# A hybrid decoder layer on one core: the norms' inverse root as one GpSimd power operation

## The chip, the core and the metric

The kernel runs on one core of one Trainium2 chip. A core has five engines that run side by side and wait for each other by semaphores: TensorE (PE in the profile; PEld is its weight load), VectorE (DVE), ScalarE (ACT), GpSimd (POOL) and SyncE (SP), which here issues the transfers. The metric is the device time of one execution in microseconds (us). Three timed executions of the kernel before gave 1698.07, 1702.21 and 1703.12 us, so a median of 1702.21 us.

## The reference

One decoder layer for 1024 tokens of width 1024, in float32. Every sub-layer starts with an RMS norm, whose reciprocal root is what the change is about:

```python
def rms_norm(x, gain):
    y = x * lax.rsqrt(jnp.mean(x * x, axis=-1, keepdims=True) + EPS)
    return y * gain
...
h = modulate(rms_norm(x, ffn1_norm), sh1, sc1)
x = x + 0.5 * g1 * swiglu(h, w_gate, w_up, w_down)           # FFN 1
h = modulate(rms_norm(x, mix_norm), sh2, sc2)
b, c, v, u = split(h @ w_in)
y_conv = b * conv3_causal(c * v)
y_ssm = glu(s5_scan(u))
x = x + g2 * (concat(rms_norm(y_conv), rms_norm(y_ssm)) @ w_out)
h = modulate(rms_norm(x, ffn2_norm), sh3, sc3)
x = x + 0.5 * g3 * swiglu(h, w_gate2, w_up2, w_down2)        # FFN 2
return rms_norm(x, final_norm)
```

The shifts, scales and gates (`sh`, `sc`, `g`) come from `silu(cond) @ w_mod + b_mod`, nine vectors of 1024.

## The kernel before

**Layout.** Activations stand transposed: 128 features on the partitions, tokens along the free axis, in two halves `h` of 512 tokens. A float32 product is made from three TensorE products of a high and a low part (`mm3`, L337): high by high, high by low, low by high. ScalarE makes the high part (a cast), VectorE the low part (a subtraction), for weights and activations alike. Most FFN products use a seven-product scheme (`seven`, `down7`); GpSimd makes the sums of weights for it (L168 to L179).

**Order of the work.** TensorE's matmuls stand in program order, and a clock counts them: each `mm3` is one tick, and work that is due later is put on the clock with `clock.after(ticks, ...)`. VectorE, ScalarE, TensorE and SyncE go through the wrapper `InOrder`, so all their instructions carry line L112 in the profile; GpSimd's carry their own lines. Within an engine the order of issue is fixed when the program is built; a scheduler decides it outside the first stage, where `InOrder.strict` holds the order as written.

**The norms.** There are thirteen roots, each for up to four groups of 128 tokens:

- `p0`, `p1`: the first norm. Tokens are on the partitions there; `root_of` (L873) makes the root of four token blocks at once, `scaled` multiplies the blocks by it on ScalarE (half 1 partly on GpSimd), `turned` transposes them on TensorE.
- `n2a`, `n2b` (before the mixer), `nAa`, `nAb`, `nBa`, `nBb` (the conv group's and the SSM group's output norm), `n3a`, `n3b` (before FFN 2) and three for the final norm, of half 0 (`n_0` in the profile, from `n4`) and of the two halves of half 1. For these, `Sumsq.rstd` (L385) puts three pieces on the clock: TensorE sums the squares over the partitions (`...st`), `roots` (L400) makes the root and `wide` (L415) spreads it over 128 columns (`...rb`); seven ticks later (11 in the final norm) TensorE brings it to all partitions (`...bc`), and the users multiply by it.

`roots` is nine VectorE instructions on 128x4 (or 128x2) elements: `v` = mean square plus epsilon; a first guess from the bits of `v` read as an integer; and seven more for two refinements, whose last leaves 8/3 of the root. `wide`, or in `root_of` one more instruction, multiplies by 0.375.

**Other work on VectorE around the norms.** The modulation vectors of later sub-layers are made beside the main work: `wm` tiles of 128x1024 come by transfer into two buffers, and VectorE reduces each with one long instruction (`mod_vector`, L437), which in the mixer's last part writes `mods` and `gate`. A buffer is loaded again only once that instruction has read it. In the stage of the output projection (`w_out`, tiles `wo`), VectorE also makes `obt` (the SSM output times its root and gain), the low parts `ob`, the updates of `x` and the low parts of the weights `w`.

**Padding.** `PAD` sets the sizes of two unused tiles at the two ends of the local memory, and with them the addresses of what lies between.

Of the kernel before, what the change touches and what calls it, by code (L numbers as in the profile page):

```python
# [21 lines left out]
P = 128  # L22
D = 1024
# [18 lines left out]
GB = G // NB  # L42


PAD = 96, 100

C_BMOD, C_N1, C_N2, C_N3, C_NF, C_ONC, C_ONS, C_CW, C_GB = 0, 72, 80, 88, 96, 104, 108, 112, 124
NCOLS = 128
# [4 lines left out]
RC2 = float(np.float32(np.round((TWO_PI - RC1) * 2.0**20) / 2.0**20))  # L53
RC3 = float(np.float32(TWO_PI - RC1 - RC2))
ROUND = 12582912.0
ROOT_BITS, ROOT_A, ROOT_B = 1595932665.0, 0.703952253, 2.38924456
EXP_C = [1.9875691500e-4, 1.3981999507e-3, 8.3334519073e-3, 4.1665795894e-2, 1.6666665459e-1, 5.0000001201e-1]


# [176 lines left out]
def hymba_layer(ctx: ExitStack, tc, x_d, xt_d, wm1_d, wmod_d, gu1_d, gs1_d, ds1_d, wl1_d, win_d, wout_d, glu_d, gu2_d, gs2_d, wd2_d, ds2_d, wl2_d, cols_d, cond_d, lam_d, bc_d, out_d):  # L236
    nc = tc.nc
    V, A, T, SP = (InOrder(tc, e) for e in (nc.vector, nc.scalar, nc.tensor, nc.sync))

    def pool(name, bufs=1, **kw):  # L240
        return ctx.enter_context(tc.tile_pool(name=name, bufs=bufs, **kw))

    pad = pool("pad")
    pad.tile([P, PAD[0]], F32, name="pad_left")
    const = pool("const", side="right")
    const.tile([P, PAD[1]], F32, name="pad_right")
    scratch = pool("scratch", space=DRAM)
# [24 lines left out]
    def t2k(name):  # L272
        return tmp.tile([P, HALF], F32, tag="t", name=name)
# [3 lines left out]
    make_identity(nc, ident[:])  # L277
    one = const.tile([P, 1], F32, name="one")
    V.memset(one[:], 1.0)
    mods = const.tile([P, 3, KT], F32, name="mods")  # L280
    scl = const.tile([P, 3, KT], F32, name="scl")
    gate = const.tile([P, 3, KT], F32, name="gate")
# [111 lines left out]

            clock.after(wait, stats)

    def roots(st, q, width, nm):

        v, y, a = (const.tile([P, 8], F32, tag=f"n{i}", name=f"{nm}n{i}", bufs=1)[:, :q] for i in "vya")
        yi = const.tile([P, 8], I32, tag="ni", name=nm + "ni", bufs=1)[:, :q]  # L400
        V.tensor_scalar(out=v, in0=st[:, :q], scalar1=1.0 / width, scalar2=EPS, op0=ALU.mult, op1=ALU.add)
        V.tensor_scalar(out=yi, in0=v.bitcast(I32), scalar1=-0.5, scalar2=ROOT_BITS, op0=ALU.mult, op1=ALU.add)
        src = yi.bitcast(F32)
        V.scalar_tensor_tensor(out=a, in0=src, scalar=-ROOT_A, in1=src, op0=ALU.mult, op1=ALU.mult)
        V.tensor_tensor(out=a, in0=a, in1=v, op=ALU.mult)
        V.scalar_tensor_tensor(out=y, in0=a, scalar=ROOT_A * ROOT_B, in1=src, op0=ALU.add, op1=ALU.mult)
        V.tensor_tensor(out=a, in0=y, in1=y, op=ALU.mult)
        V.tensor_tensor(out=a, in0=a, in1=v, op=ALU.mult)
        V.scalar_tensor_tensor(out=a, in0=a, scalar=-10.0 / 3.0, in1=a, op0=ALU.add, op1=ALU.mult)
        V.scalar_tensor_tensor(out=y, in0=a, scalar=5.0, in1=y, op0=ALU.add, op1=ALU.mult)  # L410
        return y

    widened = []
# [1 line left out]
    def wide(y, nm):  # L415

        q = y.shape[1]
        rb = t2k(nm + "rb")[:, : q * P].rearrange("p (a b) -> p a b", a=q)
        r = V.tensor_scalar(out=rb, in0=y.unsqueeze(2).to_broadcast([P, q, P]), scalar1=0.375, scalar2=None, op0=ALU.mult)
        widened.append(r)  # L420
        return rb

# [399 lines left out]
    st = t2k("st")  # L822
# [1076 lines left out]
```

## Time and profile before

| what | value |
|---|---|
| median of the runs | 1702.21 us (1698.07 to 1703.12) |
| the profiled execution's span, and its own time by the profile | 1704.7 us |
| mean granted TensorE clock in it | 0.994 |
| PE busy | 1666.8 us (98%) |
| DVE busy | 1255.5 us (74%) |
| ACT busy | 630.1 us (37%) |
| POOL busy | 382.0 us (22%) |
| share of the chain that ended last | PE 70%, DVE 8%, DMA 5% |

The page's first part gives for each engine its busy time, its share of the span and the number of its instructions. A row of the timeline reads: start, duration, engine, line, operation, output from inputs, shapes, count of merged instructions, and in brackets how long the engine had been idle before it and what it had waited for. A busy TensorE hides what the others do, so the places to look at are those where it stands idle.

### The profile page before, as it was taken

To read this page: it belongs to the slowest core of one execution; us is meant where nothing else is said; L and a number is where in the kernel's file an instruction comes from. 1 tells how busy PE (TensorE), PEld (TensorE's weight loads), DVE (VectorE), ACT (ScalarE), POOL (GpSimd) and SP (SyncE) were. 2 spreads that over 40 slices of the span, in tenths; PEclk is the share of its full clock that TensorE was granted. 3 is DMA by queue.
4 is the path that set the end of the run, shared out by engine and by line. 5 is a ranking of instruction groups with operands and counts; after the bars stand their busy time and mean duration, and the time that the engine had idled before them with its cause. 6 is when DMAs were issued, how large, how long until landed. Compare 5 with 4: busy or idle time off the path is not lost.

```text
span 1704.7 us, 20844 instructions
## 1 busy us (share of the span) xinstructions
PE 1666.8 (98%) x7545; PEld 1369.9 (80%) x7545; DVE 1255.5 (74%) x1957; ACT 630.1 (37%) x1064; POOL 382.0 (22%) x297
## 2 busy tenths in 40 slices
PE   8999999999999999999999999999999999999997
PEld 5888877788878888788777878888888888888886
DVE  7897899998589978735555857957767667576655
ACT  6525323333354332331113415434344434322233
POOL 1012222242222412100000021122333223333212
PEclk9999999999999999999999999999999999999999
DMA  8544454544665448244654232324443343759212
GB/s 350 187 148 137 172 189 155 183 149 139 213 216 170 151 152 291 70 111 149 191 151 134 70 129 112 112 74 182 188 174 148 148 173 148 269 228 381 110 50 99
DMA packets 101625, 281.48 MB, mean 165 GB/s; under 512 B 19345, under 2 KB 34961, under 8 KB 90386
## 3 DMA queue, kind: packets, MB, share of 16 engines
q1 hardware_dynamic: 101522, 280.15, 46.6%
q8 instruction: 59, 0.97, 0.2%
q14 instruction: 44, 0.36, 0.1%
HBM read 195.69 MB, written 76.02 MB: 159 GB/s over the span
## 4 chain that ended last, share of the span: by engine, by line
PE 70%; DVE 8%; DMA 5%; issue 1%; ACT 0%; SPq 0%; POOL 0%; DVEq 0%; ACTq 0%; POOLq 0%
PE wo L112 4%; PE fald L112 3%; PE fb10d L112 2%; PE u L112 2%; PE fbd_1B L112 2%; PE fbd_0B L112 2%; DMA swz<-si 2%; DVE w L112 2%; PE fad_1B L112 2%; PE b L112 2%; PE fad_0B L112 1%; PE c L112 1%; PE fb0u L112 1%; PE fad_1C L112 1%; PE fbd_1C L112 1%; PE fbd_0C L112 1%
## 5 line engine op out<-in xcount | busy, mean ns | idle before, releaser
L112 ACT CAST w<-raw 128x512 fp32r<-128x512 f32 (+1 forms) x374 | 240.9, 677 | 497.7 <-issue 72.7
L112 DVE TENSOR_TENSOR w<-raw,w 128x512 fp32r<-128x512 f32 (+1 forms) x374 | 311.2, 851 | 101.2 <-ACT w L112 100.6
L177 POOL TENSOR_TENSOR raw<-sums,raw 128x512 f32<-128x512 f32 x54 | 81.6, 1511 | 420.9 <-DVE w L112 419.9
L168 POOL TENSOR_TENSOR sums<-raw 128x512 f32<-128x512 f32 x54 | 76.4, 1415 | 308.1 <-DMA raw<-in_ds 129.1
L179 POOL TENSOR_TENSOR raw<-raw 128x512 f32<-128x512 f32 x54 | 82.3, 1526 | 86.6 <-DVE w L112 86.0
L112 DVE CUSTOM_DVE_ANT_0 wm<-wm,cact 128x1024 f32<-128x1024 f32 x56 | 77.7, 1407 | 15.1 <-DMA wm<-in_wmod 15.0
L169 POOL TENSOR_TENSOR raw<-raw 128x512 f32<-128x512 f32 x54 | 85.2, 1577 | 4.2
L370 POOL TENSOR_TENSOR n3aq<-n3aq,n3aq 128x512 f32<-128x512 f32 x5 | 7.5, 1499 | 277.4 <-ACT n3aq L112 277.2
L112 DVE TENSOR_TENSOR w<-sums,w 128x512 fp32r<-128x512 f32 x54 | 54.9, 1029 | 3.4 <-ACT w L112 2.8
L112 PE MATMUL p<-h,w 128*128 128x512 f32 x192 | 49.4, 407 | 2.0 <-ACT h L112 1.5
L112 PE MATMUL wo<-oa,w 128*128 128x512 f32 x192 | 45.5, 391 | 2.1 <-ACT w L112 1.3
L112 PE MATMUL c<-h,w 128*128 128x512 f32 x192 | 47.1, 397 | 0.0
L112 PE MATMUL v<-h,w 128*128 128x512 f32 x192 | 46.9, 395 | 0.0
L112 PE MATMUL b<-h,w 128*128 128x512 f32 x192 | 45.6, 393 | 0.0
L112 PE MATMUL wo<-ob,w 128*128 128x512 f32 x192 | 45.2, 391 | 0.0
L112 PE MATMUL u<-h,w 128*128 128x512 f32 x192 | 44.8, 392 | 0.2 <-DVE h L112 0.2
L112 PEld LDWEIGHTS wo<-oa,w 128*128 128x128 f32 x192 | 35.8, 188 | 10.2 <-ACT w L112 1.7
L112 PEld LDWEIGHTS p<-h,w 128*128 128x128 f32 x192 | 35.7, 192 | 10.1 <-ACT h L112 2.0
L112 ACT CAST w<-sums 128x512 fp32r<-128x512 f32 x54 | 32.7, 619 | 28.8 <-PE fa10gE L112 2.5
L112 PEld LDWEIGHTS u<-h,w 128*128 128x128 f32 x192 | 35.7, 188 | 8.3 <-DVE h L112 0.6
L112 PEld LDWEIGHTS wo<-ob,w 128*128 128x128 f32 x192 | 35.8, 188 | 7.4
L112 PEld LDWEIGHTS c<-h,w 128*128 128x128 f32 x192 | 35.8, 190 | 7.2
(1579 smaller groups left out, 4039.8 us busy)
## 6 DMA issues: line engine op xcount, KB each, us to landing
raw<-in_gs SPq DMA_DIRECT2D x38, 1024.0 KB, 5.0
wm<-in_wmod SPq DMA_DIRECT2D x56, 512.0 KB, 5.2
raw<-in_ds SPq DMA_DIRECT2D x16, 1024.0 KB, 6.6
mw<-in_wm SPq DMA_DIRECT2D x8, 1024.0 KB, 8.4
raw<-in_win SPq DMA_DIRECT2D x8, 1024.0 KB, 5.5
raw<-in_gu SPq DMA_DIRECT2D x6, 1024.0 KB, 4.9
raw<-in_wl SPq DMA_DIRECT2D x5, 1024.0 KB, 6.7
xb<-in_xt SPq DMA_DIRECT2D x8, 512.0 KB, 6.4
```

The source lines that it names most:

```text
L112: r = getattr(self.engine, name)(*args, **kw)
L168: self.G.tensor_tensor(out=f, in0=r[2], in1=r[1], op=ALU.subtract)
L169: self.G.tensor_tensor(out=r[1], in0=r[1], in1=r[0], op=ALU.subtract)
L177: self.G.tensor_tensor(out=r, in0=s["t3"], in1=r, op=ALU.add)
L179: self.G.tensor_tensor(out=r, in0=self.chunk(j, 3), in1=r, op=ALU.subtract)
L370: nc.gpsimd.tensor_tensor(out=a, in0=a, in1=sq[:, :n], op=ALU.add)
```

## The change

The nine instructions of `roots` become two: `v` on VectorE as before, and one GpSimd `tensor_tensor` that raises `v` to the power -0.5, with a tile of constants as its second input. The factor 0.375 in `wide` becomes 1.0. In the first norm the GpSimd instruction writes the tile that `scaled` reads, so that the tenth instruction goes too. The three working tiles that fall away and the new tile of constants are balanced by `PAD`: the tiles `w`, `h` and the other matmul operands keep their addresses, while `cols` and `ident` move by 32 bytes.

```diff
-PAD = 96, 100
+PAD = 96, 108
...
+    power = const.tile([P, 4], F32, name="power")
+    nc.gpsimd.memset(power[:], -0.5)
...
-    def roots(st, q, width, nm):
-        v, y, a = (const.tile([P, 8], F32, tag=f"n{i}", name=f"{nm}n{i}", bufs=1)[:, :q] for i in "vya")
-        yi = const.tile([P, 8], I32, tag="ni", name=nm + "ni", bufs=1)[:, :q]
+    def roots(st, q, width, nm, y=None):
+        v = const.tile([P, 8], F32, tag="nv", name=nm + "nv", bufs=1)[:, :q]
+        if y is None:
+            y = const.tile([P, 8], F32, tag="ny", name=nm + "ny", bufs=1)[:, :q]
         V.tensor_scalar(out=v, in0=st[:, :q], scalar1=1.0 / width, scalar2=EPS, op0=ALU.mult, op1=ALU.add)
-        V.tensor_scalar(out=yi, in0=v.bitcast(I32), scalar1=-0.5, scalar2=ROOT_BITS, op0=ALU.mult, op1=ALU.add)
-        src = yi.bitcast(F32)
-        V.scalar_tensor_tensor(out=a, in0=src, scalar=-ROOT_A, in1=src, op0=ALU.mult, op1=ALU.mult)
-        V.tensor_tensor(out=a, in0=a, in1=v, op=ALU.mult)
-        V.scalar_tensor_tensor(out=y, in0=a, scalar=ROOT_A * ROOT_B, in1=src, op0=ALU.add, op1=ALU.mult)
-        V.tensor_tensor(out=a, in0=y, in1=y, op=ALU.mult)
-        V.tensor_tensor(out=a, in0=a, in1=v, op=ALU.mult)
-        V.scalar_tensor_tensor(out=a, in0=a, scalar=-10.0 / 3.0, in1=a, op0=ALU.add, op1=ALU.mult)
-        V.scalar_tensor_tensor(out=y, in0=a, scalar=5.0, in1=y, op0=ALU.add, op1=ALU.mult)
+        nc.gpsimd.tensor_tensor(out=y, in0=v, in1=power[:, :q], op=ALU.pow)
         return y
...
-        r = V.tensor_scalar(out=rb, in0=y.unsqueeze(2).to_broadcast([P, q, P]), scalar1=0.375, scalar2=None, op0=ALU.mult)
+        r = V.tensor_scalar(out=rb, in0=y.unsqueeze(2).to_broadcast([P, q, P]), scalar1=1.0, scalar2=None, op0=ALU.mult)
...
     def root_of(h):
-        y = roots(st[:, 4 * h : 4 * h + 4], 4, D, f"p{h}")
         root[h] = t2k(f"py{h}")[:, :4]
-        V.tensor_scalar(out=root[h], in0=y, scalar1=0.375, scalar2=None, op0=ALU.mult)
+        roots(st[:, 4 * h : 4 * h + 4], 4, D, f"p{h}", root[h])
```

The order in which instructions stand on the engines changes at few places beyond the removed rows. Three of them matter below. The first is VectorE around the second root of the conv group (`nAb`); `yg` are the low parts of the gate's input. Before:

```order
L112 TENSOR_SCALAR nAbnv<-nAbst 128x4
L112 TENSOR_SCALAR nAbni<-nAbnv 128x4
L112 SCALAR_TENSOR_TENSOR nAbna<-nAbni 128x4
L112 TENSOR_TENSOR nAbna<-nAbna,nAbnv 128x4
L112 SCALAR_TENSOR_TENSOR nAbny<-nAbna,nAbni 128x4
L112 TENSOR_TENSOR nAbna<-nAbny 128x4
```

The three further instructions of the root follow, then seven `yg` and the widening. In the changed kernel:

```order
L111 TENSOR_SCALAR nAbnv<-nAbst 128x4
L111 TENSOR_TENSOR yg_0_7407<-yb_7256,yg_0_7407 128x512
L111 TENSOR_TENSOR yg_0_7416<-yb_7257,yg_0_7416 128x512
L111 TENSOR_TENSOR yg_0_7425<-yb_7258,yg_0_7425 128x512
L111 TENSOR_TENSOR yg_1_7479<-yb_7255,yg_1_7479 128x512
L111 TENSOR_TENSOR yg_1_7485<-yb_7256,yg_1_7485 128x512
L111 TENSOR_TENSOR yg_1_7494<-yb_7257,yg_1_7494 128x512
L111 TENSOR_TENSOR yg_1_7509<-yb_7258,yg_1_7509 128x512
L111 TENSOR_SCALAR nAbrb<-nAbny 128x512
```

The low parts `yg` now stand right behind `v`, with no part of the root between them; the widening that waits for GpSimd stays behind all seven.

The second place is VectorE behind the second root of the SSM group (`nBb`); ISA rows are the long reductions of `wm` and the short read of their sum. Before:

```order
L112 TENSOR_SCALAR nBbrb<-nBbny 128x512
L112 ISA wm_2_0_7980,mods<-wm_2_0_7980,cact_7300 128x1024
L112 ISA mods 128x1
L112 SCALAR_TENSOR_TENSOR x_0_3914<-wo_0_7644,gate,x_0_3914 128x512
L112 SCALAR_TENSOR_TENSOR x_0_3914<-wo_0_7645,gate,x_0_3914 128x512
L112 ISA wm_2_1_7982,mods<-wm_2_1_7982,cact_7300 128x1024
L112 ISA mods 128x1
L112 SCALAR_TENSOR_TENSOR obt_1_7901<-yb_7293,cols,nBbbc 128x512
```

In the changed kernel:

```order
L111 TENSOR_SCALAR nBbnv<-nBbst 128x4
L111 TENSOR_SCALAR nBbrb<-nBbny 128x512
L111 ISA wm_2_0_7906,mods<-wm_2_0_7906,cact_7262 128x1024
L111 ISA mods 128x1
L111 ISA wm_2_1_7908,mods<-wm_2_1_7908,cact_7262 128x1024
L111 ISA mods 128x1
L111 SCALAR_TENSOR_TENSOR x_0_3894<-wo_0_7588,gate,x_0_3894 128x512
L111 SCALAR_TENSOR_TENSOR x_0_3894<-wo_0_7589,gate,x_0_3894 128x512
L111 ISA wm_3_0_7911,mods<-wm_3_0_7911,cact_7262 128x1024
L111 ISA mods 128x1
L111 SCALAR_TENSOR_TENSOR obt_1_7827<-yb_7255,cols,nBbbc 128x512
```

Every reduction from here to the end of this stage stands one place earlier: three reductions instead of two stand ahead of the first `obt`. On SyncE, correspondingly, one load of `wm` stands ahead of a load of weights that it stood behind.

The third place is VectorE in the last 20 us, from the root of half 1's first piece (`n_1_0`) on; `fb10d` are the last products. Before:

```order
L112 TENSOR_SCALAR n_1_0nv<-n_1_0st 128x2
L112 SCALAR_TENSOR_TENSOR x_1_3920<-fb10d_1_256_13389,gate,x_1_3920 128x256
L112 TENSOR_SCALAR n_1_0ni<-n_1_0nv 128x2
L112 TENSOR_TENSOR x_0_3916<-x_0_3916,n_0_0bc 128x1024
L112 SCALAR_TENSOR_TENSOR n_1_0na<-n_1_0ni 128x2
L112 SCALAR_TENSOR_TENSOR x_1_3921<-fb10d_1_256_13429,gate,x_1_3921 128x256
L112 TENSOR_TENSOR n_1_0na<-n_1_0na,n_1_0nv 128x2
L112 TENSOR_TENSOR x_0_3917<-x_0_3917,n_0_0bc 128x1024
L112 SCALAR_TENSOR_TENSOR n_1_0ny<-n_1_0na,n_1_0ni 128x2
L112 SCALAR_TENSOR_TENSOR x_1_3921<-fb10d_1_256_13449,gate,x_1_3921 128x256
```

In the changed kernel:

```order
L111 TENSOR_SCALAR n_1_0nv<-n_1_0st 128x2
L111 SCALAR_TENSOR_TENSOR x_1_3900<-fb10d_1_256_13288,gate,x_1_3900 128x256
L111 TENSOR_SCALAR n_1_0rb<-n_1_0ny 128x256
L111 TENSOR_TENSOR x_0_3896<-x_0_3896,n_0_0bc 128x1024
L111 SCALAR_TENSOR_TENSOR x_1_3901<-fb10d_1_256_13319,gate,x_1_3901 128x256
L111 TENSOR_TENSOR x_0_3897<-x_0_3897,n_0_0bc 128x1024
L111 SCALAR_TENSOR_TENSOR x_1_3901<-fb10d_1_256_13339,gate,x_1_3901 128x256
L111 TENSOR_TENSOR x_1_3898<-x_1_3898,n_1_0bc 128x2x256
L111 TENSOR_SCALAR n_1_256nv<-n_1_256st 128x2
L111 TENSOR_TENSOR x_1_3899<-x_1_3899,n_1_0bc 128x2x256
L111 TENSOR_SCALAR n_1_256rb<-n_1_256ny 128x256
```

The widening of the first piece stood behind the last update of `x` before and stands two updates ahead of it now; of the four multiplications by its result one instead of two stands ahead of the second piece's `v`, and one fills the place between `v` and its widening.

TensorE's order differs in two spots: the broadcast `n2bbc` stands behind six matmuls since its sum instead of ten, and the first `wo<-ob` of half 1 are taken in an order that runs two high-by-high products ahead of the first low part.

More of the change, by code (lines that the diff above doesn't have):

```diff
@@ L55 @@
 ROUND = 12582912.0
-ROOT_BITS, ROOT_A, ROOT_B = 1595932665.0, 0.703952253, 2.38924456
 EXP_C = [1.9875691500e-4, 1.3981999507e-3, 8.3334519073e-3, 4.1665795894e-2, 1.6666665459e-1, 5.0000001201e-1]
```

## The prediction

> **What bounds the kernel now.** I read the page's engine shares first, then TensorE's idle times, then VectorE and ScalarE around each of the thirteen roots.
>
> ```profile
> core 0: 1704.7 us, clock 0.994
> PE 1666.8 (98%) x7545; PEld 1369.9 (80%) x7545; DVE 1255.5 (74%) x1957; ACT 630.1 (37%) x1064; POOL 382.0 (22%) x297
> ```
>
> TensorE sets the end: it is busy for 98% at full clock. A root matters only where TensorE stands idle because of it, and that is so in the first norm, at `nAb`, and in the final norm. At `n2b` and `nBb` it can become so. At the others (`n2a`, `nAa`, `nBa`, `n3a`, `n3b`, `n_0`) TensorE has 21 or more matmuls between sum and broadcast and never waits.
>
> **The price of the new chain.** Rows of the first norm and of GpSimd:
>
> ```profile
> 10.82 0.17 DVE L112 TENSOR_SCALAR p0nv<-st 128x4 f32<-128x4 f32 x1
> 12.86 1.71 ACT L112 ACTIVATE xb<-xb,py 128x256 f32<-128x256 f32 x4 [3.56 <-issue]
> 13.43 1.96 PE L112 MATMUL pt<-ident,xb 128*128 128x128 f32 x8 [1.76 <-ACT xb L112]
> 21.56 0.17 DVE L112 TENSOR_SCALAR p1nv<-st 128x4 f32<-128x4 f32 x1
> 23.34 0.17 DVE L112 TENSOR_SCALAR py<-p1ny 128x4 f32<-128x4 f32 x1
> 23.55 1.71 ACT L112 ACTIVATE xb<-xb,py 128x256 f32<-128x256 f32 x4 [0.22 <-DVE py L112]
> 23.69 5.59 POOL L885 TENSOR_SCALAR xb<-xb,py 128x256 f32<-128x256 f32 x4 [22.41 <-DVE py L112]
> 28.54 2.81 PE L112 MATMUL p<-h,w 128*128 128x512 f32 x11 [0.45 <-DVE h L112]
> L370 POOL TENSOR_TENSOR n_0q<-n_0q,n_0q 128x512 f32<-128x512 f32 x6 | 7.7, 1290 | 48.5 <-ACT n_0q L112 48.5
> L370 POOL TENSOR_TENSOR n_256q<-n_256q,n_256q 128x256 f32<-128x256 f32 x6 | 4.4, 737 | 4.8 <-ACT n_256q L112 4.8
> ```
>
> `py` ends at 23.51; GpSimd starts 0.18 later, ScalarE 0.04 later. With T for GpSimd's power instruction, the root is there 0.17 + 0.18 + T + 0.04 = T + 0.39 after the start of `v`, against 12.86 - 10.82 = 2.04 now. No row shows a power on GpSimd, so T is bounded: the two additions give (1290 - 737) / 256 = 2.16 ns per column and 0.18 us for the start, so four columns of an addition would take 0.19 us; that is the lower end, 0.2. As upper end I take the 128x512 addition, 1.29: a power of four columns as dear as 512 additions. For the value: a logarithm and an exponential of full float32 precision are some tens of steps where the addition is one; with fifty (my assumption) at 2.16 ns, four columns take 0.43, and with the start **T = 0.6**, nearer to the lower row.
>
> **First norm.** ScalarE, which leads TensorE here, starts on `p0` 2.04 - 0.39 - 0.6 = 1.05 earlier. On `p1` it is held only for the 0.22 in the row: its own work ends at 23.33, and the root would be there at 21.56 + 0.99 = 22.55, so these 0.22 go as well (while T is under 1.38). From 28.54 on TensorE has no gap until 137, so the shift stays: **-1.27 us**. VectorE, freed of nine instructions, follows ScalarE here and adds nothing.
>
> **n2b.** The broadcast stands behind six matmuls instead of ten:
>
> ```profile
> 719.51 1.05 PE L112 MATMUL n2bst<-one,n2bq 128*128 128x1 f32 x8 [0.98 <-DVE n2bq L112]
> 720.42 2.58 PE L112 MATMUL u<-h,w 128*128 128x512 f32 x10
> 720.60 0.16 DVE L112 TENSOR_SCALAR n2bnv<-n2bst 128x4 f32<-128x4 f32 x1 [1.14 <-PE n2bst L112]
> 722.38 0.43 DVE L112 TENSOR_SCALAR n2brb<-n2bny 128x512 f32<-128x512 f32 x1
> 722.86 1.16 PE L112 MATMUL n2bbc<-ident,n2brb 128*128 128x128 f32 x8
> ```
>
> Ten matmuls take 2.44 to the broadcast, six take 1.46, to 721.88. `rb` would end at 720.60 + 0.99 + 0.43 = 722.02: **+0.18 us** of new idle time (0 at T = 0.2, 0.87 at 1.29).
>
> **nAb.** Here the eight removed instructions stood ahead of work that TensorE waits for:
>
> ```profile
> 923.09 0.16 DVE L112 TENSOR_SCALAR nAbnv<-nAbst 128x4 f32<-128x4 f32 x1 [1.15 <-PE nAbst L112]
> 924.68 0.16 DVE L112 SCALAR_TENSOR_TENSOR nAbny<-nAbna,nAbny 128x4 f32<-128x4 f32 x1
> 925.08 4.30 DVE L112 TENSOR_TENSOR yg<-yb,yg 128x512 fp32r<-128x512 f32 x7 [0.24 <-issue]
> 925.83 9.55 PE L112 MATMUL gl<-yg,w 128*128 128x512 f32 x29 [1.73 <-DVE yg L112]
> ```
>
> TensorE idles 1.73 us for the first `yg`. In the new order it stands right behind `v`; keeping the 0.24 ahead of it, it starts at 923.25 + 0.24 = 923.49, 1.59 earlier: **-1.59 us**, whatever T is, since the widening stands behind all seven.
>
> **nBb.** This is where the change can cost. VectorE's widening waits for GpSimd with the whole engine behind it, and a third reduction, `wm_3_0`, now stands ahead of `obt`:
>
> ```profile
> 964.12 0.16 DVE L112 TENSOR_SCALAR nBbnv<-nBbst 128x4 f32<-128x4 f32 x1 [3.16 <-PE nBbst L112]
> 966.24 1.22 DVE L112 CUSTOM_DVE_ANT_0 wm<-wm,cact 128x1024 f32<-128x1024 f32 x1
> 969.95 2.06 DVE L112 SCALAR_TENSOR_TENSOR obt<-yb,cols,nBbbc 128x512 f32<-128x512 f32 x3
> 971.93 1.89 DVE L112 TENSOR_TENSOR ob<-obt,ob 128x512 fp32r<-128x512 f32 x3
> 973.16 5.60 PE L112 MATMUL wo<-ob,w 128*128 128x512 f32 x24
> 984.16 4.48 DMA wm<-in_wmod
> 988.78 1.23 DVE L112 CUSTOM_DVE_ANT_0 wm<-wm,cact 128x1024 f32<-128x1024 f32 x1 [3.50 <-DMA wm<-in_wmod]
> 997.31 3.44 DVE L112 TENSOR_TENSOR w<-raw,w 128x1024 fp32r<-128x1024 f32 x2
> 998.44 1.63 PE L112 MATMUL wo<-oa,w 128*128 128x512 f32 x6 [1.32 <-ACT w L112]
> 1000.80 3.49 PE L112 MATMUL wo<-oa,w 128*128 128x512 f32 x14 [0.74 <-DVE w L112]
> ```
>
> `rb` can start at 964.12 + 0.99 = 965.11, and `wm_2_0` 0.34 later at 965.45, 0.79 earlier than now. Only when it has read its buffer (965.45 + 1.22 = 966.7) can that buffer be loaded for `wm_3_0`; by the 4.48 of the load shown, that lands at 971.2, and with the reduction `obt` starts at 972.4, 2.4 later than now. The first low part `ob`, now ready at about 972.6, would be ready near 975; TensorE, which is there at 973.16 and can run two high products (0.45) first, idles some 1.4 us. That is not all lost: the 1.32 + 0.74 us at 998 exist because the weights' low parts stand behind reductions that wait for loads. From here to there the new order again holds one more load-and-reduce step (4.48 + 1.22), partly behind work that TensorE releases; following the two buffers step by step I get TensorE's last release at 1001.2 instead of 1000.80. So **+0.4 us**, between -0.6 and +1.4 if each of the last two loads lands half a us sooner or later; with T it moves one for one.
>
> **Final norm.** Two broadcasts on the path to the end:
>
> ```profile
> 1686.42 0.95 PE L112 MATMUL n_0st<-one,n_0q 128*128 128x1 f32 x8
> 1687.49 0.15 DVE L112 TENSOR_SCALAR n_0nv<-n_0st 128x2 f32<-128x2 f32 x1
> 1691.85 0.47 DVE L112 SCALAR_TENSOR_TENSOR x<-fb10d,gate,x 128x256 f32<-128x256 f32 x1
> 1692.35 0.42 ACT L112 ACTIVATE n_256q<-x 128x256 f32<-128x256 f32 x1 [0.52 <-DVE x L112]
> 1693.42 0.71 PE L112 MATMUL n_0bc<-ident,n_0rb 128*128 128x128 f32 x4 [2.35 <-DVE n_0rb L112]
> 1695.38 0.15 DVE L112 TENSOR_SCALAR n_256nv<-n_256st 128x2 f32<-128x2 f32 x1
> 1697.21 0.29 DVE L112 TENSOR_SCALAR n_256rb<-n_256ny 128x256 f32<-128x256 f32 x1
> 1697.55 1.22 PE L112 MATMUL n_256bc<-ident,n_256rb 128*128 128x128 f32 x4 [2.63 <-DVE n_256rb L112]
> ```
>
> The first piece's broadcast no longer comes behind VectorE's last update of `x`, so it runs right behind the last matmul and the second piece's sum need not wait for it. VectorE's row of long work in between keeps its length: it loses four small instructions and gains the widening, so the last update starts only about 0.2 earlier, 1691.65, and its square ends at 1692.6. The sum starts there; `v` follows 1687.49 - 1686.42 = 1.07 later, at 1693.7, and `rb` 0.99 later, at 1694.7 against 1697.21: **-2.5 us**. The multiplications and stores behind it are unchanged.
>
> **Sum.** -1.27 + 0.18 - 1.59 + 0.4 - 2.5 = -4.8 us on the profiled 1704.7, so 1699.9. The runs' median lies 2.5 below the profiled execution, so I forecast **1697.4 us**. At T = 0.2 the terms give -1.67, 0, -1.59, 0, -2.9 = -6.2 (1696.0); at T = 1.29 they give -0.58, +0.87, -1.59, +1.1, -1.8 = -2.0 (1700.2). The gain is gone near T = 1.8.
>
> **Rivals.**
>
> *A slow power: slower than before.* If GpSimd works through the power in several hundred steps per column, T is several us, and every root on the path waits for it. It decides from T = 1.8. At T = 3: `p0` loses 1.35 and `p1` 1.4 (root at 24.95, not 23.55), `n2b` 2.54, `nBb` 2.8, the tail gains only 0.1, `nAb` still gains 1.59: +6.4, so 1708.6. For it: no row shows a power, and an addition of 512 columns already takes 1290 ns. Against it: four columns are little work. Chance 0.13.
>
> *A first use that costs extra.* The first power stands in the first norm, where it is exposed. If its code had to be fetched from memory, that is one transfer more on the path; by the `wm` load's 4.48 as upper end and nothing as lower, the sum comes to between -4.8 and -0.3, with half of it 1699.6. Against it:
>
> ```profile
> 74.56 1.29 POOL L168 TENSOR_TENSOR sums<-raw 128x512 f32<-128x512 f32 x1 [45.27 <-issue]
> ```
>
> the first addition of the program takes what the later ones take. The Trainium skill (GPSIMD Engine Reference, section Instruction dispatch) says that the first call of a freshly loaded kernel pays about 6 us with no instruction shown; by that the sum would be +1.2. The addition's row does not bear it out for its own operation; no row can show it for the power. Chance 0.07.
>
> *The early gains are absorbed at 998.* The weights there wait for loads; if those do not move with TensorE, the 2.7 us won before are lost and only the tail's 2.5 remain: 1699.7. Against it: the loads are released by VectorE's reductions, which follow TensorE. Chance 0.07.
>
> *The reordering at nBb is free* (loads land quicker, the third reduction ends ahead of need) and T is near 0.2: -6.5, 1695.7. Chance 0.11.
>
> **How the numbers follow.** The forecast has 0.62. What a measurement here can tell from no change is about 0.3%, 5.1 us; the forecast's -2.0 to -6.2 lies on both sides of it, so of its 0.62 I put 0.32 on faster and 0.30 on no difference. The free reordering gives 0.10 and 0.01, the first use and the absorbed gain 0.14 on no difference, the slow power 0.13 on slower: faster 0.42, same 0.45, slower 0.13. The forecast's own range is 1696.0 to 1700.2; the runs spread by +0.9 and -4.1 about their median, and the upper end goes part of the way to the slow power: 1692.5 to 1704.5.
>
> **What would show it.** GpSimd's power rows give T at once. Right: ScalarE's `xb` start near 11.8, the 1.73 at `gl` nearly gone, an idle time of 1 to 2 us ahead of `wo<-ob` near 971, a smaller one near 998, and the last `rb` about 2.5 us earlier against the last matmul. Wrong: a power over 1.3 us, a first power longer than the others, or no new idle time at `nBb`.

## Result and profile after

| | before | after |
|---|---|---|
| median of the runs, us | 1702.38 (11 runs, 1698.07 to 1707.01) | 1698.36 (11 runs, 1697.15 to 1702.11) |
| ratio of after to before | | 0.9979, 95% interval 0.9970 to 0.9989 |
| profiled execution's span, us | 1704.7 | 1698.9 |

The change takes 0.21% off, about 3.6 us (1702.4 x 0.0021); the medians lie 4.0 apart. The interval leaves out 1, and it lies within the 0.3% that the prediction took as what can be told from no change; of its three outcomes the likeliest came. Here and below, medians and ratios leave out four executions that took far longer than the rest (1936.80, 2807.49, 4300.37 and 4329.98 us).

The page of the changed kernel, its granted clock and its engine shares:

```profile
core 0: 1698.9 us, clock 0.995
PE 1664.2 (98%) x7545; PEld 1368.2 (81%) x7545; DVE 1238.9 (73%) x1851; ACT 629.9 (37%) x1064; POOL 396.5 (23%) x311
```

VectorE has 106 instructions fewer, GpSimd 14 more (thirteen powers and the constant). The price that the prediction could only bound stands in GpSimd's groups of instructions (busy time, mean ns of one, idle time before it):

```profile
L404 POOL TENSOR_TENSOR py<-p0nv,power 128x4 f32<-128x4 f32 x1 | 1.0, 1017 | 10.4 <-DVE p0nv L111 10.4
L404 POOL TENSOR_TENSOR nBany<-nBanv,power 128x4 f32<-128x4 f32 x1 | 1.3, 1319 | 17.6 <-DVE nBanv L111 17.6
L404 POOL TENSOR_TENSOR n_256ny<-n_256nv,power 128x2 f32<-128x2 f32 x1 | 0.7, 707 | 1.7 <-DVE n_256nv L111 1.7
```

T is 1.02 us for four columns and 0.71 for two, not 0.6 (the ten other powers take 1.01 to 1.04 and 0.71). The first power of the program (`p0nv`) takes as long as the later ones: the rival of a first use that costs extra is out, and so is the slow power, which decides from 1.8.

The places that the prediction named, in the timeline of the changed kernel (start, us, engine, operation, count, idle time ahead of it):

```profile
11.33 0.17 DVE L111 TENSOR_SCALAR p0nv<-st 128x4 f32<-128x4 f32 x1
12.70 1.71 ACT L111 ACTIVATE xb<-xb,py 128x256 f32<-128x256 f32 x4 [2.93 <-POOL py L404]
14.78 1.04 ACT L111 CAST w<-raw 128x1024 fp32r<-128x1024 f32 x1 [0.37 <-DMA raw<-in_gu]
28.43 2.83 PE L111 MATMUL p<-h,w 128*128 128x512 f32 x11 [0.22 <-DVE h L111]
...
721.02 1.16 PE L111 MATMUL n2bbc<-ident,n2brb 128*128 128x128 f32 x8 [0.30 <-DVE n2brb L111]
...
922.26 8.21 PE L111 MATMUL gl<-yg,w 128*128 128x512 f32 x33
...
958.24 0.95 PE L111 MATMUL nBbst<-one,nBbq 128*128 128x1 f32 x8
960.56 0.43 DVE L111 TENSOR_SCALAR nBbrb<-nBbny 128x512 f32<-128x512 f32 x1 [1.18 <-POOL nBbny L404]
965.79 1.99 DVE L111 CUSTOM_DVE_ANT_0 wm<-wm,cact 128x1024 f32<-128x1024 f32 x1 [1.19 <-DMA wm<-in_wmod]
967.71 2.05 DVE L111 SCALAR_TENSOR_TENSOR obt<-yb,cols,nBbbc 128x512 f32<-128x512 f32 x3
969.15 0.73 PE L111 MATMUL wo<-ob,w 128*128 128x512 f32 x2 [0.54 <-ACT ob L111]
970.42 5.29 PE L111 MATMUL wo<-ob,w 128*128 128x512 f32 x22 [0.54 <-DVE ob L111]
975.06 2.01 ACT L111 CAST w<-raw 128x1024 fp32r<-128x1024 f32 x2 [2.18 <-PE wo L111]
995.58 1.65 PE L111 MATMUL wo<-oa,w 128*128 128x512 f32 x6 [1.52 <-ACT w L111]
...
1689.07 0.38 PE L111 MATMUL n_256st<-one,n_256q 128*128 128x1 f32 x2 [0.36 <-POOL n_256q L371]
1690.52 0.16 DVE L111 TENSOR_SCALAR n_256nv<-n_256st 128x2 f32<-128x2 f32 x1 [0.78 <-PE n_256st L111]
1691.50 0.29 DVE L111 TENSOR_SCALAR n_256rb<-n_256ny 128x256 f32<-128x256 f32 x1 [0.22 <-POOL n_256ny L404]
1691.85 1.19 PE L111 MATMUL n_256bc<-ident,n_256rb 128*128 128x128 f32 x4 [1.36 <-DVE n_256rb L111]
```

Two rows of the kernel before, for the comparison at `nBb`:

```profile
963.14 0.95 PE L112 MATMUL nBbst<-one,nBbq 128*128 128x1 f32 x8
978.12 1.06 ACT L112 CAST w<-raw 128x1024 fp32r<-128x1024 f32 x1 [2.99 <-PE wo L112]
```

From `v` (11.33) to ScalarE's `xb` (12.70) are now 1.37 us, before 2.04; but in this execution the tokens came 0.5 later (`v` started at 10.82 before), so TensorE is only 0.11 earlier at 28.43. At `nAb` the 1.73 of idle time are gone: `gl` runs through. At `nBb` the late reduction stands ahead of `obt`, and TensorE waits twice 0.54 for `ob`. In the final norm the 2.35 ahead of `n_0bc` are gone, and the 2.63 ahead of `n_256bc` became 1.36.

To see a term of 1 us when whole spans differ by several, I cut each profiled execution at rows that all kernels have (the start of one row minus the start of another, in the timelines) and compare the stretches. The kernels below the second are the experiments, told further down; `x<-x,n_256bc` are the last multiplications:

| kernel | start to `p<-h` | `nAbst` to `nBbst` | `nBbst` to `n_0st` | `n_0st` to `x<-x,n_256bc` |
|---|---|---|---|---|
| before (VectorE) | 28.54 | 41.14 | 714.85 | 20.82 |
| after (GpSimd) | 28.43 | 36.89 | 716.94 | 17.89 |
| root on GpSimd in the final norm only | 28.49 | 38.47 | 715.46 | 17.92 |
| root on GpSimd in `nAa`, `nAb` only | 28.91 | 36.90 | 714.94 | 22.00 |
| root on GpSimd in `p0`, `p1` only | 28.09 | 38.44 | 715.08 | 21.00 |
| root on GpSimd in `nBa`, `nBb` only | 28.90 | 40.10 | 716.96 | 21.63 |
| root on GpSimd everywhere but `nBa`, `nBb` | 28.03 | 36.89 | 716.16 | 17.92 |
| root on GpSimd everywhere but there and `n2a`, `n2b` | 27.86 | 36.88 | 716.18 | 17.72 |
| after, reductions kept in place at `nBb` | 28.08 | 36.89 | 715.01 | 17.72 |
| after, each power twice | - | 36.89 | 717.90 | 18.89 |

Two of these, 716.16 and 716.18, hold something else: in the one the granted clock falls to 0.56 and 0.87 in the slices from 993 to 999, in the other TensorE idles 1.13 us at 1565.59 for VectorE's `w`, in FFN 2. The stretches that are not listed (first norm to `n2bst`, `n2bst` to `nAbst`) differ by up to 6 us between kernels whose order of work is the same there.

### The profile page after: what moved, and what is told of

It is laid out like the page before. It is cut to its first block, busy times and chain, and to the rows that moved or that the text cites. A ratio compares the mean times of both kernels' runs of the same rounds, so it can differ in the third digit from the quotient of the medians.

```text
span 1698.9 us, 20768 instructions
## 1 busy us (share of the span) xinstructions
PE 1664.2 (98%) x7545; PEld 1368.2 (81%) x7545; DVE 1238.9 (73%) x1851; ACT 629.9 (37%) x1064; POOL 396.5 (23%) x311
## 4 chain that ended last, share of the span: by engine, by line
PE 72%; DVE 7%; DMA 4%; issue 1%; POOL 0%; SPq 0%; ACT 0%; DVEq 0%; POOLq 0%; ACTq 0%
PE fald L111 3%; PE wo L111 3%; PE fb10d L111 2%; PE fbd_1B L111 2%; PE fbd_0B L111 2%; PE u L111 2%; DMA swz<-si 1%; DVE w L111 1%; PE b L111 1%; PE fad_0B L111 1%; PE fad_1B L111 1%; PE fb0u L111 1%; PE fbd_1C L111 1%; PE fbd_0C L111 1%; PE fbd_1A L111 1%; PE fbd_0A L111 1%
## 5 line engine op out<-in xcount | busy, mean ns | idle before, releaser
L111 PEld LDWEIGHTS b<-h,w 128*128 128x128 f32 x192 | 35.5, 188 | 7.2
```

The lines of the kernel that those rows point to most:

```text
L111: r = getattr(self.engine, name)(*args, **kw)
```

## Experiments

Most experiments have one kernel as base, the changed one with the eight VectorE operations kept beside the power; a list of names says which roots use which, and the padding is set so that matmul operands keep their places:

```diff
-PAD = 96, 108
+PAD = 96, 92
+POWER = ("n4_0_0", "n4_1_0", "n4_1_256")
...
+        if nm in POWER:
+            nc.gpsimd.tensor_tensor(out=y, in0=v, in1=power[:, :q], op=ALU.pow)
+            return y
...
```

Behind the last line the eight operations of the kernel before follow, unchanged. In the two experiments on the order at `nBb` and on a longer power, the list names all thirteen roots.

**Final norm alone** (the list above).

> The GpSimd root only in the final norm (three roots), the eight VectorE operations in the ten others. By the step-by-step theory with the measured power (0.71 us at 128x2) the tail alone gives 2.4 us, by the two traces 2.9 us (the last matmul to the last multiplication): 1699.5 to 1700.0 against 1702.4. The rival, that the whole gain of 4 us comes from the final norm and the gains and costs ahead of it cancel, expects 1698.4.

Measured: 1698.03 against 1702.9 (30 runs), ratio 0.9972 [0.9962, 0.9981], -4.8 us. The stretch from `n_0st` to the last multiplication is 17.92, as in the changed kernel, against 20.82 to 22.00 in the five kernels with the VectorE root there. On the whole time it is worth more than the two traces had it: the interval (-6.5 to -3.2) leaves out the two lower of the three numbers expected (-2.4 and -2.9) and holds the rival's -4.0. The rival's sum is borne out by what follows: the gains and costs ahead of the final norm, seen one by one below, come to 0.1 us together.

**`nAa` and `nAb` alone** (`POWER = ("nAa", "nAb")`).

> The GpSimd root only in the conv group's output norm (nAa and nAb). The prediction's own step expects the removed idle time alone, -1.6 us at nBbst. The clock theory expects more there, -3.9: the kernel before runs 29 matmuls behind the idle time of 1.73 us in 9.55 us, which at the pace of the changed kernel (32 in 7.98) would be 7.23, so 2.3 us go with the clock that falls to 0.50 to 0.73. A third theory, that the weights' loads at 998 absorb what is won ahead of them, expects no difference behind 1000.8. On the whole time: 1700.8, 1698.5 or 1702.4.

Measured: 1701.44 against 1702.9, 0.9990 [0.9980, 1.0000]: -1.7 us. The stretch `nAbst` to `nBbst` is 36.90, and 38.47 or 38.44 in the two kernels that have the VectorE root and a full clock there: -1.56, the prediction's -1.59. The -4.25 between the traces of before and after was the clock. Slices of 3 us of before (start:end, length, busy us and count of TensorE, of its weight loads, of VectorE, ScalarE and GpSimd, granted clock, DMA share, GB/s):

```profile
924.00:927.00 3.00, 1.27 (x4) 0.98 (x4) 2.62 (x9) 0.25 (x1) 0.00 (x0) 0.63 0.94 344
927.00:930.00 3.00, 3.00 (x9) 2.32 (x8) 2.72 (x5) 0.00 (x0) 0.00 (x0) 0.50 0.58 218
930.00:933.00 3.00, 3.00 (x12) 2.36 (x11) 0.00 (x0) 0.00 (x0) 0.00 (x0) 0.73 0.00 0
```

The same slices, and the row of `gl`, of the kernel with the GpSimd root in the final norm alone, which has the VectorE root and the 1.73 us of idle time here as before has:

```profile
924.00:927.00 3.00, 1.28 (x6) 1.07 (x7) 2.66 (x8) 0.14 (x1) 0.00 (x0) 1.00 0.99 355
927.00:930.00 3.00, 3.00 (x15) 2.47 (x14) 2.62 (x5) 0.00 (x0) 0.00 (x0) 1.00 0.52 205
```

```profile
925.72 6.88 PE L113 MATMUL gl<-yg,w 128*128 128x512 f32 x29 [1.73 <-DVE yg L113]
```

The same 29 matmuls after the same idle time take 9.55 us in the one execution and 6.88 in the other. So the clock did fall in before's profile, but not because of the idle time's length alone: of five executions with 1.73 to 1.84 us there, two show it (9.55 here, 8.51 in the kernel with `nBa` and `nBb` alone). My clock theory's -3.9 for this edit falls; of the -4.25, 1.6 is the change's, the rest one execution's luck.

**Fillers in the idle time.** The kernel before with two matmuls into unused columns of the tile of sums:

```diff
-                st = sm([P, 4], self.name + "st")
+                st = sm([P, HALF], self.name + "st")
                 self.sums(st)
+                if self.name == "nAb":
+                    for _ in range(2):
+                        T.matmul(st[:, P : P + 320], lhsT=ident[:], rhs=self.parts[0][:, :320], start=True, stop=True)
...
```

Further lines hold the `yg` behind the root, where the kernel before has them.

> The kernel before with all its VectorE roots; only two matmuls of 128x320 stand behind the sums of nAb, into columns that nobody reads, so that TensorE's idle time of 1.73 us shrinks to about 0.7 with every other instruction in its old place. The clock theory expects gl<-yg behind it at about 0.25 us for one instead of 0.33, and nBbst about 2.3 us earlier although nothing was removed (some 1700.1). The rival, that the slow matmuls of the kernel before had another reason (a neighbour's traffic, operands), expects 0.33 us for one as before and no gain (1702.4).

Measured: 1703.35 against 1702.9, 1.0002 [0.9990, 1.0014]. It does not tell the theories apart, because the idle time did not shrink: VectorE's `v` waited for the fillers too (it starts 2.28 us behind `nAbst`, 1.09 in the kernel before), so `yg` came 1.2 us later and TensorE still idled 1.84. The 29 matmuls behind it took 6.91, at full clock.

**Everything but `nBa` and `nBb`.**

> The GpSimd root everywhere but in the SSM group's output norm (nBa and nBb keep the eight VectorE operations, and VectorE's order there is that of the kernel before). If the change costs 2.05 us between nBbst and the end of that stage, as the two traces have it (-4.90 becomes -2.85), this kernel is 2 us below the changed kernel, 1696.3. If the difference there is not the root's but comes from the loads that do not move with TensorE, it equals the changed kernel, 1698.4, and the idle times ahead of wo<-oa near 998 grow instead.

Measured: 1696.11 against 1702.9, 0.9963 [0.9950, 0.9976], -6.3 us; the median is where the first theory had it. The idle times ahead of `wo<-ob` are gone, the one at 993.38 has 2.08 us instead of 1.52, and the clock falls behind it; so its stretch reads 716.16. That idle time has grown, as the rival expects, but not by the gains ahead of it: in the best list below, which has the same gains there, it is 1.23.

**`nBa` and `nBb` alone.**

> The GpSimd root only in nBa and nBb, with the reductions standing one step earlier behind nBb as in the changed kernel. By the order theory this place costs 2.0 us by itself: nBbst to the first n_0st takes 716.9 instead of 714.9, the whole is 1704.3 against 1702.3 of the kernel before. The rival, that the 2 us exist only together with the earlier gains (because the loads do not move with TensorE), expects 714.9 and no difference.

Measured: 1706.15 against 1703.12, 1.0018 [1.0007, 1.0029], +3.1 us. The stretch is 716.96, against a mean of 714.98 in five that have the order of before (714.85, 715.46, 714.94, 715.08, and 714.55 in the kernel with fillers): the place costs 2.0 us by itself, whatever comes ahead of it. With the two kernels whose stretch holds something else the mean is 715.32 and the cost 1.6. Nearer to the place the profiles agree more closely: ScalarE's first cast of weights behind `ob` starts 14.97 or 14.98 behind `nBbst` in all eight with the order of before, and 16.82 or 16.83 in all four with the new order and a single power, 1.85 later.

**The order or the wait?** The whole change with three reductions tied to their old places:

```diff
+BEHIND = {(6, 5): "x1_0", (6, 6): "obt3_1", (6, 7): "ob3_1"}
...
         mod_vector(r, dst[:, d : d + 1])
+        if (n, d) in BEHIND:
+            V.follow(reduced[-1], marks[BEHIND[n, d]])
```

> The whole change, with three edges of order added: the reductions wm_2_1, wm_3_0 and wm_3_1 behind nBb stay behind the x update, behind obt and behind ob, where the kernel before has them. VectorE still waits for GpSimd's power at nBbrb. If the 2 us at nBb come from the reduction that stands ahead of obt, nBbst to the first n_0st takes 714.9 us as in the kernel before (716.9 in the changed kernel), the idle times ahead of wo<-ob near 970 are gone, and the whole is 1696.1 as with the VectorE root there. If they come from VectorE's standing wait for the power (1.13 us at nBbrb), the whole stays near 1698.4 and nBbst to n_0st near 716.9.

Measured: 1698.13 against 1702.32, 0.9975 [0.9964, 0.9986]. The median alone would speak for the second theory; its interval, from 1696.2 to 1700.0, holds the second and ends at the first. The stretch does tell: 715.01. Its timeline at the place:

```profile
960.59 0.43 DVE L114 TENSOR_SCALAR nBbrb<-nBbny 128x512 f32<-128x512 f32 x1 [1.19 <-POOL nBbny L408]
965.06 2.06 DVE L114 SCALAR_TENSOR_TENSOR obt<-yb,cols,nBbbc 128x512 f32<-128x512 f32 x3 [0.44 <-PE nBbbc L114]
968.28 5.60 PE L114 MATMUL wo<-ob,w 128*128 128x512 f32 x24
973.24 1.06 ACT L114 CAST w<-raw 128x1024 fp32r<-128x1024 f32 x1 [2.99 <-PE wo L114]
993.75 1.64 PE L114 MATMUL wo<-oa,w 128*128 128x512 f32 x6 [1.50 <-ACT w L114]
```

VectorE stands for the power as in the changed kernel (1.19), but `obt` starts 6.80 behind `nBbst` (at 958.26 here) instead of 9.47, and TensorE goes on without a gap. So the 2 us are the reduction's that moved ahead of `obt`, not the wait's for GpSimd. In the whole time the place shows when it is added alone (+3.1, above). Whether the kept order wins it back there stays open: this kernel's median is 2.0 us above that of the kernel without `nB`, where by the stretches the two should be equal, and the intervals are too wide to say more.

**The price of a longer power.** Each power is made twice:

```diff
+            nc.gpsimd.tensor_tensor(out=a, in0=v, in1=power[:, :q], op=ALU.pow)
             nc.gpsimd.tensor_tensor(out=y, in0=v, in1=power[:, :q], op=ALU.pow)
```

> The whole change with each power made twice on GpSimd (the first result is not used), everything else in its order: T goes from 1.02 to about 2.04 us at 128x4 and from 0.71 to 1.42 at 128x2. By the prediction's formula the first norm loses 1.0, n2b 1.0, nBb 1.0 and the last norm 0.7, together +3.7 us: 1702.1. The rival, that a later root ahead of 998 is absorbed by the weights' wait there, expects the tail's 0.7 alone: 1699.1. At nAb both expect nothing: VectorE goes on with yg during the power.

Measured: 1706.83 against 1702.32, 1.0025 [1.0015, 1.0035]: 8.5 us above the changed kernel by the medians and 7.8 by the ratios, not 3.7. Term by term: `n2bbc` waits 1.29 instead of 0.30 (+1.0), `nBbst` to `n_0st` +0.96, the final norm +1.0, `nAbst` to `nBbst` 36.89 as before (0). These are as expected, but for 0.3 more in the final norm: there the last root is 0.67 later behind `v`, and `v` itself 0.50 later, since VectorE stands 0.42 for the root before. The first norm is not as expected: TensorE comes to `fa2gC` at 126.95 instead of 122.59, +4.4 instead of +1.0. Timeline there:

```profile
12.61 1.34 DVE L113 CUSTOM_DVE_ANT_0 mw<-mw,cact,pre 128x1024 f32<-128x1024 f32 x1 [0.92 <-DMA mw<-in_wm]
12.83 1.99 POOL L408 TENSOR_TENSOR py<-p0nv,power 128x4 f32<-128x4 f32 x1
14.86 1.71 ACT L113 ACTIVATE xb<-xb,py 128x256 f32<-128x256 f32 x4 [4.88 <-POOL py L408]
23.66 1.34 DVE L113 CUSTOM_DVE_ANT_0 mw<-mw,cact,pre 128x1024 f32<-128x1024 f32 x1
23.84 2.04 POOL L407 TENSOR_TENSOR p1na<-p1nv,power 128x4 f32<-128x4 f32 x1 [9.01 <-DVE p1nv L113]
```

A power that starts beside a reduction of VectorE (`mw`) takes 2.0 us, not 1.0: it ends about 0.9 us after the reduction does. So `p0`'s root comes 2.2 us later (ScalarE's `xb` at 14.86 instead of 12.70), `p1`'s comes too late for ScalarE as well (`xb` waits 1.78 for it), and `p<-h`, at 27.70 in the changed kernel, starts at 31.26. Then the clock falls to 0.57 and 0.86 from 30 to 36. Its earlier fall, 0.80, 0.50 and 0.56 from 15 to 24, is no cause: the changed kernel has 0.66, 0.50 and 0.70 there. In the changed kernel `p1`'s power starts at 22.16 and the reduction at 22.23: it escapes by 0.07 us.

**The first norm alone** (`POWER = ("p0", "p1")`).

> The GpSimd root only in the first norm (p0, p1). By the prediction's formula with the measured T of 1.02 us, p0 gives 0.63 and p1 0.22, together -0.85 us. The rival, that the loads of x, of the weights and the modulation behind it set the end of this stage, expects 0.1 to 0.3, as the two traces have it where p<-h starts at 28.54 and 28.43. On the whole 1702.0 or 1702.7, with before at 1702.9.

Measured: 1701.19 against 1702.32, 0.9989 [0.9979, 0.9998]: -1.9 us, between -3.6 and -0.3. `p<-h` starts at 28.09. Over all profiles it starts at 28.80 in the mean of the five kernels with the VectorE root (28.49 to 29.18, the one with fillers among them) and at 28.05 in the mean of the seven with a single GpSimd power (27.75 to 28.43, with the last two kernels of this section): -0.75. Part of the spread is the tokens' arrival (`p0nv` starts between 10.73 and 11.48). Counted from `p0nv`, `p<-h` starts 17.70 to 17.72 later in the five and 17.00 to 17.10 in the seven: -0.67, where the formula has -0.85 and the rival -0.1 to -0.3.

The way there is not the formula's. In the changed kernel `xb` of `p0` starts 0.67 earlier behind `p0nv` than before, but ScalarE's next row, a cast of weights, only 0.21 earlier (3.45 instead of 3.66): it waits 0.37 for their load, as the rival has it. `p1` brings this to 0.39 at ScalarE's cast of `h` (15.70 instead of 16.09), and the rest comes from VectorE's low part of `h`, which takes 0.69 instead of 0.92. The shift stays: at `fa4gC` near 215 the means are 214.71 and 215.77.

**The best list** (`p0`, `p1`, `nAa`, `nAb`, `n3a`, `n3b` and the final norm).

> The GpSimd root only where it was seen to gain or to cost nothing: p0, p1, nAa, nAb, n3a, n3b and the final norm. By the sum of the parts as the traces show them (first norm -0.7, nAb -1.6, final norm -2.9 to -4.0) -5.2 to -6.3 us against the kernel before: 1696.0 to 1697.1, 0.3 below the kernel that has it at n2a and n2b too, and 1.3 to 2.4 below the changed kernel. If the parts do not add up, it stays near the changed kernel's 1698.4.

Measured: 1697.04 against 1703.12, 0.9960 [0.9947, 0.9973]. It and the kernel that leaves out only `nB` are the two fastest, -6.8 and -6.3 us by ratio, in line with the sum of the parts; one from the other they cannot be told. Their intervals and the changed kernel's (0.9979 [0.9970, 0.9989]) overlap at the edges, so the 2 us between them are likely, not certain.

**The operation by itself.** Behind the last norm, a row of operations on GpSimd over constants:

```diff
+    for n in (1, 2, 4, 8, 16, 64, 512):
+        for dst, op in ((pw, ALU.pow), (sm_, ALU.add), (pr, ALU.mult)):
+            GP.tensor_tensor(out=dst[:, :n], in0=base[:, :n], in1=ex[:, :n], op=op)
...
```

> The changed kernel with, behind its last norm, a row of operations on GpSimd over constants: power, addition and multiplication at 1, 2, 4, 8, 16, 64 and 512 columns, and at 4 columns the power with exponent 2 and with a base of 1000. From the two sizes in the changed kernel (0.71 at two columns, 1.01 at four) a power takes 0.40 us and 0.153 us per column: 0.55 at 1, 1.62 at 8, 2.85 at 16, 10.2 at 64 and 78.7 at 512; the addition by 0.18 us and 2.16 ns per column 0.19 at 4. If a power's time goes in steps of a few columns, 1 column takes as long as 2 and the slope falls behind 8. The whole time means nothing here.

GpSimd's timeline in it:

```profile
1691.52 0.55 POOL L1819 TENSOR_TENSOR bpow<-bbase,bexp 128x1 f32<-128x1 f32 x1
1693.28 1.01 POOL L1819 TENSOR_TENSOR bpow<-bbase,bexp 128x4 f32<-128x4 f32 x1
1699.70 10.55 POOL L1819 TENSOR_TENSOR bpow<-bbase,bexp 128x64 f32<-128x64 f32 x1
1710.78 82.16 POOL L1819 TENSOR_TENSOR bpow<-bbase,bexp 128x512 f32<-128x512 f32 x1
1796.05 1.02 POOL L1821 TENSOR_TENSOR bpow<-bbase,bexp 128x4 f32<-128x4 f32 x1
```

A power takes 0.39 us and (82.16 - 0.55) / 511 = 0.160 us for each column, a little more than the 0.153 expected from two sizes, without steps (0.70 at two columns, 1.64 at eight); exponent 2 (the last row) and a base of 1000 (1.01) change nothing. One column of it is worth some 70 of an addition's 2.16 ns, and the start is twice the addition's.

**Power beside VectorE.** Four powers of 128x4 alone, beside eight additions of two tiles, beside eight multiplications by a constant, and beside eight reductions on VectorE:

```diff
+        for _ in range(4):
+            GP.tensor_tensor(out=out[:, :4], in0=left[:, :4], in1=ex[:, :4], op=ALU.pow)
+        for _ in range(8):
+            if stage == "add":
+                DV.tensor_tensor(out=res[:], in0=left[:], in1=right[:], op=ALU.add)
...
```

> The changed kernel with, behind its last norm, four rows of four powers of 128x4 on GpSimd: alone, beside additions of two tiles on VectorE, beside multiplications by a constant on VectorE, and beside reductions of two tiles on VectorE (the operation that builds the modulations). If GpSimd and VectorE shut each other out of memory while an operation reads two tiles, the power takes 1.0 alone and beside the multiplications and up to 1.7 to 2.0 us beside the additions and reductions, as the powers of 1.99 and 2.04 us in the first norm of the doubled kernel do. If these were slow for another reason, all four rows show 1.0. The whole time means nothing here.

The four rows of GpSimd, in that order, and VectorE's beside the second:

```profile
1691.63 4.27 POOL L1820 TENSOR_TENSOR gpow<-vleft,gexp 128x4 f32<-128x4 f32 x4
1696.57 5.87 POOL L1820 TENSOR_TENSOR gpow<-vleft,gexp 128x4 f32<-128x4 f32 x4
1703.10 5.10 POOL L1820 TENSOR_TENSOR gpow<-vleft,gexp 128x4 f32<-128x4 f32 x4
1708.86 5.91 POOL L1820 TENSOR_TENSOR gpow<-vleft,gexp 128x4 f32<-128x4 f32 x4
```

```profile
1696.52 5.78 DVE L1823 TENSOR_TENSOR vout<-vleft,vright 128x512 f32<-128x512 f32 x8 [1.03 <-POOL vleft L1818]
```

One power takes 1.07 (the kernel's last multiplications still run beside this row), 1.47, 1.28 (the multiplications by a constant end 1.5 us before the powers) and 1.48 us. VectorE does slow it, beside all three kinds; the expectation that a multiplication by a constant would leave it alone was wrong. Four powers (4.27) and eight additions (0.69 each) went through together in 5.9 us, where one after the other they would take 9.8, so the two don't take turns for the whole of an instruction.

## Why the prediction was right, and where it was off

The forecast was 1697.4 (own range 1696.0 to 1700.2), the median is 1698.36. On the profiled execution it was 1699.9, and the span is 1698.9, but that nearness means less: before's own profile held a fall of the clock at `nAb`, worth 2.7 us (9.55 - 6.88), that the forecast did not see in the rows. Term by term, by the stretches:

| term | forecast, us | measured, us | what settles it |
|---|---|---|---|
| first norm | -1.27 | -0.67 | `p0nv` to `p<-h`, 17.71 to 17.04, means of five and seven |
| `n2b` | +0.18 | +0.30 | idle ahead of `n2bbc` |
| `nAb` | -1.59 | -1.56 | 38.45 to 36.89 |
| `nBb` | +0.4 | +2.0 | 714.98 to 716.95 |
| final norm | -2.5 | -2.9 to -4.1 | 20.82 to 22.00 against 17.89 |
| sum | -4.8 | -2.9 to -4.1 | by the ratio of the runs: -3.6 |

So the kind of every term was right, and the sum's nearness is in part luck: the first norm and `nBb` came out worse by 0.6 and 1.6, the final norm better by 0.4 to 1.6. Ahead of the final norm the measured terms cancel (-0.67 + 0.30 - 1.56 + 2.0 = 0.1); the whole gain is the final norm's.

**T was mis-sized: 0.6, measured 1.02** (0.71 at two columns). The step that failed is "with fifty (my assumption) at 2.16 ns": the slope is 0.160 us a column, not 0.108, and the start 0.39, not 0.18. Both bounds held. The doubled power shows how it enters: one for one at `n2b` and `nBb`, somewhat more in the tail (1.0 for 0.7), not at `nAb`, as the prediction had it. With 1.02 its formula gives -0.85 for the first norm, 0.2 from the measured -0.67, but by another way: most of `p0`'s gain ends at ScalarE's wait for a load of weights, which the prediction's path lacks. It gives +0.60 for `n2b`, of which 0.30 came: `rb` starts 1.29 after `v` (719.24 to 720.53), where the formula has T + 0.39 = 1.41, and the six matmuls ahead of the broadcast took 1.66 (719.06 to 720.72, where the idle 0.30 begin), not 1.46.

**`nAb` was right to 0.03 us**, independent of T, as it said; `nAa` and `nAb` alone and the doubled power show it.

**`nBb` was the real miss: +0.4 with -0.6 to +1.4 about it, measured +2.0.** The first half held: a new idle time ahead of `wo<-ob` near 970, forecast some 1.4 us, measured 2 x 0.54, with `ob`'s low product at 12.18 behind `nBbst` (970.42 - 958.24) instead of 10.47 (973.16 - 963.14, and two matmuls of 0.45), 1.71 later. That this came near has some luck in it: the load of `wm_3_0` landed 3.7 us after its buffer was read (962.13 to 965.79) instead of 4.48, and the reduction, beside an addition on GpSimd, took 1.99 instead of 1.22. The step that failed is "That is not all lost", by which the waits at 998 would take up most of it. They took up nothing: 1.52 and 0.72 us stand there, before 1.32 and 0.74. The loads at which those weights wait are not on a time of their own. ScalarE's cast at 975.06 waits for TensorE (2.18 behind `wo`), 16.82 after `nBbst` instead of 14.98 (978.12 in before); the low parts, the reductions and the next loads follow it. When TensorE is late at `ob`, the whole chain to 998 is late by as much: in the doubled power the low product comes 0.99 later still (13.17), the cast 0.98 later (17.80), and the two waits are 1.54 and 0.71. The same fact put down the rival of gains absorbed at 998: the stretch behind `nBbst` is as long whether the gain ahead of it is there (714.94, 715.01) or not (714.85, 715.08). The rival of a free reordering is out too; its -6.5 was 0.3 more than the terms that it names give (-1.67 - 1.59 - 2.9 = -6.2). That the reordering and not the wait for GpSimd is the cost is shown by the kept order (715.01).

**Final norm: right in kind, short by 0.4 where the clock does the same.** In before and after it is slow at the last broadcast alone (1.22 and 1.19). There `v` of the last piece starts 15.34 behind the `n_0st` of half 0 instead of 17.39 (1690.52 - 1675.18, 1695.38 - 1677.99), 0.37 better than the forecast's 1.68: VectorE's last update starts 0.36 earlier, not "only about 0.2", and `v` follows it after 1.84 instead of 2.05. From `v` to `rb` it is 0.98 instead of 1.83; the forecast's 0.99 is luck, since T is 0.11 longer (0.71) and the two handovers are as much shorter than the 0.22 of the formula (0.08 and 0.03). What the forecast lacked is the clock: with two idle times of 2.2 to 2.7 us ahead of its broadcasts, the VectorE root leaves TensorE slow from `n_0bc` on (1.22 instead of 0.71) in three of five executions (stretches of 21.63 to 22.00), from the sums on in a fourth (21.00) and at the last broadcast alone in the fifth (20.82). With the GpSimd root it is slow at the last broadcast in three of five, and before it in none. Timeline and slices of the kernel with the GpSimd root in `nA` only:

```profile
1687.10 1.22 PE L113 MATMUL n_0bc<-ident,n_0rb 128*128 128x128 f32 x4 [2.72 <-DVE n_0rb L113]
1688.11 1.71 PE L113 MATMUL n_256st<-one,n_256q 128*128 128x1 f32 x8
```

```profile
1687.00:1690.00 3.00, 2.72 (x12) 2.63 (x12) 1.47 (x4) 0.00 (x0) 0.00 (x0) 0.50 0.04 17
```

The eight sums take 1.71 at a clock of 0.50; at full clock, in before, they took 0.95. In the mean over five profiles each (without the doubled power and the two that go on with other work on GpSimd) the stretch goes from 21.42 to 17.83, -3.6. The whole time of this edit alone, -4.8 [-6.5, -3.2], is in keeping with that; no run separates the clock's part.

## What to carry to other kernels

Before an operation moves to an idle engine, look at what the scheduler moves with it: here the operation itself cost what its bounds said, TensorE's only new wait for a root was 0.30 us at `n2b`, and the one reduction that slipped ahead of the waiting work cost 2 us. A wait that looks like slack (here at 998) is slack only if what it waits for is not itself released by the engine that was late. Compare two traces by stretches between common rows and look at the granted clock in each before a difference is given to the change.

## What the runs showed of the hardware

**The clock falls after short idle times, in some executions and not in others.** Behind 1.73 us of idle time at `nAb` the clock fell in the one execution (0.63, 0.50, 0.73 in three slices of 3 us, together 3.4 us of full clock lost, so 6.8 us at half) and not in the other; around `n2bst`, where TensorE idles 0.98 to 1.00 and makes eight small sums, five of the thirteen profiles show it. The kernel without `nB`, slices at `n2bst`:

```profile
720.00:723.00 3.00, 2.93 (x13) 2.20 (x12) 0.43 (x1) 0.00 (x0) 0.56 (x1) 0.55 0.02 5
723.00:726.00 3.00, 3.00 (x13) 2.44 (x13) 2.81 (x5) 2.03 (x3) 0.00 (x0) 0.88 0.00 0
```

That is (0.45 + 0.12) x 3 = 1.7 us lost, 3.4 us at half speed. The Trainium skill (TensorE: Matmul & The Clock Gate, section Part 1: The HAM clock gate) has a free-running window of about 3.4 us that decides between half and full clock; the lengths of 3.4 and 6.8 us and the chance agree with it (in the kernel with `nBa` and `nBb` alone, 0.79 and 0.64 behind the 1.73 us, it is 1.7 us lost and 3.4 at half). It also has the clock fall after at least one idle window of that length; here 1.0 to 1.73 us of idle time were enough.

**GpSimd and VectorE hold each other up.** A power of 1.0 us takes 1.3 to 1.5 in the mean beside rows of additions, multiplications by a constant or reductions on VectorE, 1.07 beside the kernel's last multiplications, and 2.0 if a reduction of 1.34 us has just begun; in the changed kernel `nBa`'s takes 1.32. The other way round, the widening `n_256rb`, 0.29 us, takes 1.05 and 1.51 in the two kernels where GpSimd fills constants beside it. The Trainium skill (SBUF — State Buffer, section SBUF: two separate sides) says that the two engines share a pair of ports as an exclusive lock for a whole instruction. That a power waits for the end of a reduction that began first agrees. Not in agreement with "whole" are the four powers and eight additions that fit into 5.9 us, and `p1`'s power in the changed kernel, 1.01 long, beside a reduction that begins 0.07 after it and still takes only 1.35.
